# A slice's operand and weight loads in two pools by first need, gated second-stage loads, and last norms over 1024 columns

## The chip, the cores and the metric

One core of one Trainium2 chip runs the whole program. The metric is the device time of one execution in microseconds, median of the runs. TensorE multiplies, VectorE (DVE) and ScalarE (ACT) do elementwise work, GpSimd (POOL) and SyncE (SP) issue DMAs, each on a queue of its own.

## The reference

A block of a streaming encoder over 512 rows of 2048 columns in float32, one layer:

```python
h = layer_norm(x, ln_in_g, ln_in_b)
u = h @ W_in                                   # pool values | q | k | v
mix = concat(multi_scale_pool(u), stick_breaking_attention(q, k, v)) @ W_out
h = layer_norm(ALPHA * h + mix, ln1_g, ln1_b)
f = relu(h @ W_1 + b_1) ** 2                   # 2048 -> 8192, "FFN1"
f = f @ W_2 + b_2                              # 8192 -> 2048, "FFN2"
h = layer_norm(ALPHA * h + f, ln2_g, ln2_b)
```

## The kernel before

Float32 products are made of rounded parts: a matrix is split into a high part `th` (a cast on ACT, L756) and a low part `tl` (a subtract on DVE, L757), and three matmuls stand for one.

FFN1 runs in 16 blocks of 512 columns (`f0` to `f15`). `operands` squares each block's four PSUM banks on DVE into one tile `g` (`r15_0` to `r15_3` are the last block's activations), makes sums and differences of its quarters, and splits them into `fh` (ACT, L699) and `fl` (DVE, L700). POOL's queue stores them to a scratch in DRAM, `f_d[slice][unit]`, four stores of 896 KB a block (L702). Seven operands, numbered 0 to 6, come out of each block.

FFN2 runs in 4 slices (`slice_of`) of 4 units (blocks) each, as a product of two-by-two blocks with seven multiplications. In a slice the steps `one` and `five` go over units 0 and 1, then 2 and 3; then `six` and `three_` over the units, then `seven`, then `four` and `two`. Each step does two column halves (n = 0, 1), and one step of one unit and half is 12 matmuls of 128x512. Step one multiplies operand 0, five operand 3, six 4, three_ 6, seven 5, four 2 and two 1. Steps one, six, seven and four add into the PSUM banks `x`, five and three_ into `v`. In the traces a tile's name has lost its digits of slice and kind: `o` is any operand, `b` any raw unit of w2.

- Operands: `operand` (L735) loads 512 KB from `f_d` on SP's queue into a place of a ring of 16: four in pool `first`, twelve in `ring`. `o0_4_1` is slice 0, operand 4, unit 1.
- Weights: `w2_unit` (L746) loads 512 KB of w2 on SP's queue into one of ten raw places, three in `wp` and seven in `right`; they are called b11, b12, b22 and b21 by the quarter they come from. In slice 0 three units of step one take b11 and five adds b12 to it on DVE (L808, giving `c`); for the other units a chain `c` is loaded with b11 (L797), split for step one, and b12 is added in DRAM-to-SBUF by an accumulating DMA on POOL's queue (`add_unit`, L750). In six DVE adds b22 to the chain (L817), and three_ adds b12 to the raw tile by POOL's queue.
- The tile scheduler sets each engine's order from priorities (`tc.high_priority`) and the waits that pools imply. A queue runs in order: what is behind a waiting load waits too. A DMA of SP also waits for the one eight places before it.
- Pools `chains`, `right` and `ring` are opened after FFN1's pools are closed and lie over their space, so a first tile in them waits for the last readers of what lay there.

After each stage `every` adds PSUM to the accumulators `acc0` to `acc3` on DVE (L772). At the end `norm_out` normalizes each 128-row block `tb`: statistics (L928), then for each of four 512-column quarters one instruction with mean and scale (L932), one with the reciprocal deviation and bias (L933), and an output DMA (L934).

Of the kernel before, what the change touches and what calls it, by code (L numbers as in the profile page):

```python
# [9 lines left out]
F32 = mybir.dt.float32  # L10
F32R = mybir.dt.float32r
AF = mybir.ActivationFunctionType
ALU = mybir.AluOpType

P = 128
N = 512
# [7 lines left out]
def block_kernel(  # L24
# [18 lines left out]
    nc = tc.nc  # L43
# [4 lines left out]
    NT = S // P  # L48
    NQ = D // N
# [5 lines left out]
    out2 = out[0]  # L55
# [3 lines left out]
    def pool(stack, name, bufs, **kw):  # L59
        return stack.enter_context(tc.tile_pool(name=name, bufs=bufs, reuse_waits="tile", **kw))  # L60
# [6 lines left out]
    wp = pool(ctx, "wp", 2)  # L67
# [17 lines left out]
    def f(ap):  # L85
        return ap.bitcast(F32)

    def after(ins, earlier):

        tc.add_manual_dep(ins.ins, earlier.ins.name, mybir.DependencyInfo(  # L90
            mybir.DependencyClass.Sync, mybir.DependencyReason.DATA), reason="whole bank")
# [4 lines left out]
    def rows_tile(i, name, dt=F32):  # L96
        return rows.tile([P, NQ, N], dt, tag=f"y{i}", name=name)
# [182 lines left out]
    def three(bank, a, b, first, last, free=False):  # L280
        (ah, al), (bh, bl) = a, b
        for n, (l, r) in enumerate(((ah, bh), (ah, bl), (al, bh))):
            mm = nc.tensor.matmul(bank, l, r, start=first and n == 0, stop=last and n == 2, skip_group_check=free)  # L283
        return mm
# [246 lines left out]
    for half in range(2):  # L531
        if half:
            v_block(half)
        for pair in (2 * half, 2 * half + 1):
            parts = qk_block(pair)
# [6 lines left out]
    acc_t = [rows_tile(tb, f"acc{tb}") for tb in range(NT)]  # L542
    acc = [[acc_t[tb][:, q, :] for q in range(NQ)] for tb in range(NT)]
# [107 lines left out]
    for q in range(NQ):  # L651
        gb = tmp.tile([P, N], F32, tag="w", bufs=3, name=f"g1_{q}")
# [5 lines left out]
        for tb in range(NT):  # L658
            a = acc[tb][q]
# [11 lines left out]
    first = pool(ctx, "first", 4, side="right")  # L671
# [7 lines left out]
    f_d = [[scratch.tile([OPS, 2, P, N], F32, name=f"f_d{s}_{u}") for u in range(PER)] for s in range(NS)]  # L679
# [30 lines left out]
    late = ctx.enter_context(ExitStack())  # L710
    chains = pool(late, "chains", 1)
    right = pool(late, "right", 2)
    ring = pool(late, "ring", 12)
    ps = pool(late, "ps", 2, space=PSUM)
    used = {"op": 0, "raw": 0, "parts": 0}

    def turn(what, own, n):

        used[what] += 1
        return (used[what] - 1) % n < own  # L720

    def place(name, dt=F32R):

        at_first = turn("op", 4, 16)
        return (first if at_first else ring).tile([P, 2, N], dt, tag="o", bufs=4 if at_first else 12, name=name)

    rowsop = {}

    def operand(s, us, *os):

        with tc.high_priority(offset=400):
            for u in us:
                for o in os:
                    t = place(f"o{s}_{o}_{u}")
                    nc.sync.dma_start(f(t), f_d[s][u][o].rearrange("h p t -> p h t"))  # L735
                    rowsop[o, u] = t.rearrange("p h (i t) -> p h i t", i=2)

    def w2_at(b, half, q):

        k0 = b * N + half * H2  # L740
        return w2[k0:k0 + H2, q * N:(q + 1) * N].rearrange("(c p) n -> p c n", p=P)

    def w2_unit(b, half, q, name):
        early_one = turn("raw", 3, 10)
        raw = (wp if early_one else right).tile([P, 2, N], F32, tag="raw", bufs=3 if early_one else 7, name=name)
        nc.sync.dma_start(raw, w2_at(b, half, q))  # L746
        return raw

    def add_unit(t, b, half, q):
        nc.gpsimd.dma_start(t, w2_at(b, half, q), accum_op=ALU.add)  # L750

    def parts(t, name, ring=False):
        pl = wp if turn("parts", 2, 4) else right
        h = place(f"th_{name}") if ring else pl.tile([P, 2, N], F32R, tag="wh", bufs=2, name=f"th_{name}")
        l = place(f"tl_{name}") if ring else pl.tile([P, 2, N], F32R, tag="wl", bufs=2, name=f"tl_{name}")
        nc.scalar.copy(h, t)  # L756
        nc.vector.tensor_tensor(l, t, f(h), op=ALU.subtract)  # L757
        return h, l

    def times(banks, op, u, w, first, last, ts=(0, 1)):  # L760
        a, (wh, wl) = rowsop[op, u], w
        for i in range(2):
            for t in ts:
                ts_ = slice(t * P, (t + 1) * P)
                mm = three(banks[t], (a[:, 0, i, ts_], a[:, 1, i, ts_]), (wh[:, i, :], wl[:, i, :]),
                           first and i == 0, last and i == 1, True)
        return mm
# [9 lines left out]
    def slice_of(s):  # L777
# [2 lines left out]
        ahead = lambda: tc.high_priority(offset=400)  # L780
        units = range(PER)
        x = [pair(f"x{s}_{n}", f"x{n}") for n in range(2)]
        chain, b22, b11 = {}, {}, {}

        def step(n, u):
            return s * PER + u, f"{s}_{n}_{u}", (u == 0, u == PER - 1)
# [1 line left out]
        def one(n, u):  # L788
            b, at, e = step(n, u)
            with ahead():  # L790
                if s == 0 and 2 * u + n < 3:

                    b11[n, u] = w2_unit(b, 0, n, f"b11_{at}")
                    p1 = parts(b11[n, u], f"1_{at}")
                else:
                    c = chain[n, u] = chains.tile([P, 2, N], F32, tag=f"c{n}{u}", bufs=1, name=f"c_{at}")
                    nc.sync.dma_start(c, w2_at(b, 0, n))  # L797
                    p1 = parts(c, f"1_{at}")
                    add_unit(c, b, 0, n + 2)
            times(x[n], 0, u, p1, *e)  # L800

        def five(n, u):
            b, at, e = step(n, u)
# [8 lines left out]
        def six(n, u):  # L812
            b, at, _ = step(n, u)
            with ahead():
                b22[n, u] = w2_unit(b, 1, n + 2, f"b22_{at}")
                c = chain[n, u]
                nc.vector.tensor_tensor(c, c, b22[n, u], op=ALU.add)  # L817
                p6 = parts(c, f"6_{at}")
                if end:
                    add_unit(c, b, 1, n)  # L820
            times(x[n], 4, u, p6, False, u == PER - 1)
# [54 lines left out]
        every(x, 0, 0)  # L876
        every(v, 2, 2)
        for u in units:
            operand(s, (u,), 4, 6)
            both(six, (u,))  # L880
            both(three_, (u,))
        every(x, 0, 2)
# [31 lines left out]
    gb = {}  # L914

    def load_vectors():

        for n, vec in (("g", ln2_g[0]), ("b", ln2_b[0])):
            for i in range(2):
                t = place(f"ln2{n}{i}", F32)  # L920
                nc.sync.dma_start(t, vec.rearrange("(i q n) -> i q n", i=2, n=N)[i].partition_broadcast(P))
                for j in range(2):
                    gb[n, 2 * i + j] = t[:, j, :]

    def norm_out(tb):
        st = small.tile([P, NQ, 6], F32, name=f"st2_{tb}", tag="st")
        for q in (2, 3, 0, 1):
            nc.vector.bn_stats(st[:, q, :], acc[tb][q])  # L928
        mu, rs = finish_stats(st, f"n2{tb}", const)
        for q in range(NQ):  # L930
            a = acc[tb][q]
            nc.vector.scalar_tensor_tensor(a, a, mu, gb["g", q], op0=ALU.subtract, op1=ALU.mult)  # L932
            nc.vector.scalar_tensor_tensor(a, a, rs, gb["b", q], op0=ALU.mult, op1=ALU.add)  # L933
            nc.sync.dma_start(out2[tb * P:(tb + 1) * P, q * N:(q + 1) * N], a)  # L934

    for s in range(NS):
        slice_of(s)
# [33 lines left out]
```

## Time and profile before

| | us |
|---|---|
| median of three runs | 1992.52 |
| the three runs | 1992.07, 1992.52, 2177.56 |
| the profiled execution | 1992.84 |
| its span on the core | 1991.1 |
| TensorE busy in it | 1929.6 |

The page gives each engine's busy time and the share of the span. The trace gives each instruction's start and length, the idle time before it and what ended that, and the DMA issues with the time from issue to landing. A chain of waits follows the end of the program back, at each step to what released it.

### The profile page before, as it was taken

The numbers are of one execution on the slowest core, as the hardware profiler recorded it, in microseconds if no ns is written. First come the engines' busy times: TensorE is split into PE (matmuls) and PEld (weight loads), VectorE is DVE, ScalarE is ACT, GpSimd is POOL, SyncE is SP. The second block draws the span as 40 slices with busy tenths as digits, with TensorE's granted clock in tenths as the row PEclk, the third lists the DMA queues.
The fourth block names the chain that finished last, engine by engine and source line by source line (L and its number), as shares of the span: only waits on it lengthen the run. The fifth ranks groups of instructions, "written<-read, shape, count | busy, mean of one in ns | idle before, by whom it ended". The sixth has DMA issues, their size and how long they took to land.

```text
span 1991.1 us, 22343 instructions
## 1 busy us (share of the span) xinstructions
PE 1929.6 (97%) x8736; PEld 1596.0 (80%) x8736; DVE 1143.1 (57%) x1444; ACT 737.1 (37%) x898; POOL 168.4 (8%) x175
## 2 busy tenths in 40 slices
PE   6999999999999999999999999995999999999997
PEld 4888888887888988888888888873888888888885
DVE  8445565666458744444444444453666676675768
ACT  3344555552124233333333333331333333333341
POOL 5000000000000000000100000010101101100230
PEclk8999999999999999999999999996999999999999
DMA  6122222235344365555555555579788888888792
GB/s 223 33 85 85 74 86 84 76 105 184 107 148 122 130 219 180 170 169 169 203 205 184 169 169 169 170 259 356 179 290 226 189 275 239 184 264 274 184 218 85
DMA packets 171562, 345.48 MB, mean 174 GB/s; under 512 B 10688, under 2 KB 28224, under 8 KB 171072
## 3 DMA queue, kind: packets, MB, share of 16 engines
q1 hardware_dynamic: 137184, 249.07, 38.2%
q0 software_dynamic: 34128, 94.90, 18.1%
q8 instruction: 69, 1.13, 0.2%
q14 instruction: 37, 0.30, 0.1%
q10 hardware_dynamic: 144, 0.07, 0.0%
HBM read 281.09 MB, written 62.91 MB: 173 GB/s over the span
## 4 chain that ended last, share of the span: by engine, by line
PE 94%; DVE 3%; DMA 1%; SPq 1%; issue 1%; ACT 0%; DVEq 0%; ACTq 0%
PE f L210 33%; PE x L283 16%; PE qk L361 9%; PE v L283 9%; PE o L210 7%; PE p L210 4%; PE w L283 4%; PE o L283 3%; PE f L283 2%; PE v L210 2%; PE z L283 1%; PE v L276 1%; DMA o<-f_d 1%; PE v L274 1%; PE v L273 1%
## 5 line engine op out<-in xcount | busy, mean ns | idle before, releaser
L210 PE MATMUL f<-h1h,wh_f 128*128 128x512 f32 x960 | 373.5, 389 | 0.0
L210 PE MATMUL f<-h1l,wh_f 128*128 128x512 f32 x960 | 373.5, 389 | 0.0
L283 PE MATMUL x<-th,o 128*128 128x512 f32 x1024 | 325.8, 393 | 24.9 <-DMA o<-f_d 24.5
L210 PE MATMUL f<-h1h,wl_f 128*128 128x512 f32 x960 | 349.1, 389 | 0.0
L184 DVE TENSOR_TENSOR wl_f<-raw_f,wh_f 128x1024 fp32r<-128x1024 f32 x120 | 146.9, 1224 | 325.0 <-ACT wh_f L183 325.0
L183 ACT CAST wh_f<-raw_f 128x1024 fp32r<-128x1024 f32 x120 | 126.4, 1053 | 392.4 <-PE f L210 374.2
L283 PEld LDWEIGHTS x<-th,o 128*128 128x128 f32 x1024 | 193.3, 189 | 68.6 <-DMA o<-f_d 24.9
L757 DVE TENSOR_TENSOR tl<-c,th 128x1024 fp32r<-128x1024 f32 x125 | 152.2, 1224 | 130.2 <-ACT th L756 129.5
L756 ACT CAST th<-c 128x1024 fp32r<-128x1024 f32 x125 | 130.7, 1052 | 232.8 <-PE x L283 139.6
L210 PEld LDWEIGHTS f<-h1h,wh_f 128*128 128x128 f32 x960 | 180.3, 188 | 37.3
L210 PEld LDWEIGHTS f<-h1h,wl_f 128*128 128x128 f32 x960 | 180.2, 188 | 37.4
L210 PEld LDWEIGHTS f<-h1l,wh_f 128*128 128x128 f32 x960 | 180.2, 188 | 37.3
L283 PE MATMUL x<-tl,o 128*128 128x512 f32 x512 | 201.1, 393 | 0.3 <-DVE tl L757 0.3
L283 PE MATMUL v<-th,o 128*128 128x512 f32 x512 | 164.6, 395 | 3.1 <-ACT th L756 3.1
L756 ACT CAST th<-b 128x1024 fp32r<-128x1024 f32 x99 | 104.2, 1053 | 158.9 <-PE v L283 66.2
L757 DVE TENSOR_TENSOR tl<-b,th 128x1024 fp32r<-128x1024 f32 x99 | 120.7, 1222 | 70.0 <-ACT th L756 69.9
L702 POOL DMA_DIRECT2D f_d<-fh x32 | 30.9, 977 | 1193.6 <-ACT fh L699 1193.6
L283 PEld LDWEIGHTS v<-th,o 128*128 128x128 f32 x512 | 97.2, 190 | 25.0 <-ACT th L756 4.0
L283 PEld LDWEIGHTS x<-tl,o 128*128 128x128 f32 x512 | 96.6, 189 | 21.8 <-DVE tl L757 0.7
L283 PE MATMUL v<-tl,o 128*128 128x512 f32 x256 | 100.9, 394 | 0.0
L361 PE MATMUL qk<-hTl,wh_qk 128*128 128x512 f32 x256 | 99.9, 390 | 0.0
L361 PE MATMUL qk<-hTh,wh_qk 128*128 128x512 f32 x256 | 99.5, 390 | 0.0
(206 smaller groups left out, 3070.4 us busy)
## 6 DMA issues: line engine op xcount, KB each, us to landing
raw_f<-in_w_ff_dram SPq DMA_DIRECT2D x120, 512.0 KB, 3.9
o<-f_d SPq DMA_DIRECT2D x112, 512.0 KB, 6.4
b<-in_w_ff_dram SPq DMA_DIRECT2D x70, 512.0 KB, 5.5
f_d<-fh POOLq DMA_DIRECT2D x32, 896.0 KB, 6.0
f_d<-fl POOLq DMA_DIRECT2D x32, 896.0 KB, 9.6
c<-in_w_ff_dram POOLq DMA_DIRECT2D x37, 512.0 KB, 10.4
raw_qk<-in_w_in_dram SPq DMA_DIRECT2D x64, 256.0 KB, 2.9
b<-in_w_ff_dram POOLq DMA_DIRECT2D x32, 512.0 KB, 8.6
```

The costliest lines, as they stand in the source:

```text
L183: nc.scalar.copy(h, raw)
L184: nc.vector.tensor_tensor(l, raw, f(h), op=ALU.subtract)
L210: mm = nc.tensor.matmul(bank, a, b, start=first and n == 0, stop=last and n == 2)
L273: nc.tensor.matmul(bank, xh[kc][:, ts_], wh[n], start=n == 0, stop=False)
L274: nc.tensor.matmul(bank, xl[kc][:, ts_], wh[n], start=False, stop=False)
L276: mm = nc.tensor.matmul(bank, xh[kc][:, ts_], wl[n], start=False, stop=n == last)
L283: mm = nc.tensor.matmul(bank, l, r, start=first and n == 0, stop=last and n == 2, skip_group_check=free)
L361: nc.tensor.matmul(bank, a, b, start=kc == 0 and n == 0, stop=kc == KC - 1 and n == 2)
L702: nc.gpsimd.dma_start(f_d[b // PER][b % PER][:, n, :, i * H2:(i + 1) * H2].rearrange("o p t -> p o t"), f(t))
L756: nc.scalar.copy(h, t)
L757: nc.vector.tensor_tensor(l, t, f(h), op=ALU.subtract)
```

## The change

1. The place of an operand is taken from `first` (4), `ring_a` (4) and `ring_b` (8) instead of `first` (4) and `ring` (12); that of a raw unit from `wp` (3), `right` (3) and `raw_b` (4) instead of `wp` (3) and `right` (7). The number of places and their turn are the same; what they lie over is not.
2. In slice 0 the loads of six and three_ for unit u (operands 4 and 6, and b22) wait until the last matmul of the (4+u)-th step of one, in the order of the units and halves of `begun`: `begun[4]` and `[5]` are unit 2, `[6]` and `[7]` unit 3.
3. The last norms run over 1024 columns at a time, and all of the first instruction's pieces come ahead of the second's. Each block's output leaves in two DMAs, the last block's in four as before.

Lines of the changed kernel: L741 is L735 before, L754 is L746, L767 is L757, L807 is L797, L818 is L808, L827 is L817, L782 is L772, L937 is L928, L941 is L932 and L945 is L933.

```diff
     right = pool(late, "right", 2)
-    ring = pool(late, "ring", 12)
+    ring_a = pool(late, "ring_a", 4)
+    raw_b = pool(late, "raw_b", 4)
+    ring_b = pool(late, "ring_b", 8)
...
-    def turn(what, own, n):
-
+    def turn(what, *homes):
+
+        at = used[what] % sum(n for _, n in homes)
         used[what] += 1
-        return (used[what] - 1) % n < own
+        for home, n in homes:
+            if at < n:
+                return home, n
+            at -= n

     def place(name, dt=F32R):

-        at_first = turn("op", 4, 16)
-        return (first if at_first else ring).tile([P, 2, N], dt, tag="o", bufs=4 if at_first else 12, name=name)
+        home, n = turn("op", (first, 4), (ring_a, 4), (ring_b, 8))
+        return home.tile([P, 2, N], dt, tag="o", bufs=n, name=name)
...
-    def operand(s, us, *os):
+    def operand(s, us, *os, behind=None):
...
-                    nc.sync.dma_start(f(t), f_d[s][u][o].rearrange("h p t -> p h t"))
+                    load = nc.sync.dma_start(f(t), f_d[s][u][o].rearrange("h p t -> p h t"))
+                    if behind:
+                        after(load, behind)
...
-    def w2_unit(b, half, q, name):
-        early_one = turn("raw", 3, 10)
-        raw = (wp if early_one else right).tile([P, 2, N], F32, tag="raw", bufs=3 if early_one else 7, name=name)
-        nc.sync.dma_start(raw, w2_at(b, half, q))
+    def w2_unit(b, half, q, name, behind=None):
+        home, places = turn("raw", (wp, 3), (right, 3), (raw_b, 4))
+        raw = home.tile([P, 2, N], F32, tag="raw", bufs=places, name=name)
+        load = nc.sync.dma_start(raw, w2_at(b, half, q))
+        if behind:
+            after(load, behind)
...
-            times(x[n], 0, u, p1, *e)
+            begun.append(times(x[n], 0, u, p1, *e))
...
-                b22[n, u] = w2_unit(b, 1, n + 2, f"b22_{at}")
+                b22[n, u] = w2_unit(b, 1, n + 2, f"b22_{at}", begun[4 + u] if s == 0 else None)
...
-            operand(s, (u,), 4, 6)
+            operand(s, (u,), 4, 6, behind=begun[4 + u] if s == 0 else None)
...
-        for q in range(NQ):
-            a = acc[tb][q]
-            nc.vector.scalar_tensor_tensor(a, a, mu, gb["g", q], op0=ALU.subtract, op1=ALU.mult)
-            nc.vector.scalar_tensor_tensor(a, a, rs, gb["b", q], op0=ALU.mult, op1=ALU.add)
-            nc.sync.dma_start(out2[tb * P:(tb + 1) * P, q * N:(q + 1) * N], a)
+        for i in range(2):
+            a = acc_t[tb][:, 2 * i:2 * i + 2, :]
+            nc.vector.scalar_tensor_tensor(a, a, mu, gb["g", i], op0=ALU.subtract, op1=ALU.mult)
+        for i in range(2):
+            for j in range(2) if tb == NT - 1 else [slice(0, 2)]:
+                a, b = acc_t[tb][:, 2 * i:2 * i + 2, :][:, j], gb["b", i][:, j]
+                nc.vector.scalar_tensor_tensor(a, a, rs, b, op0=ALU.mult, op1=ALU.add)
+                to = out2[tb * P:(tb + 1) * P, :].rearrange("p (i j n) -> p i j n", i=2, n=N)[:, i]
+                nc.sync.dma_start(to[:, j], a)
```

SP in slice 0, before, from the last of FFN2's early loads to the operands of one and five for units 2 and 3 (`o0_0_2` to `o0_3_3`); the loads of b22, b21 and operand 5 above them have no reader until later stages (L746 and L735 as above):

```order
L735 DMA o0_5_1_10345<-f_d0_1_5518 128x2x512
L746 DMA b22_0_1_2_10170<-in_w_ff2_dram 128x2x512
L746 DMA b21_0_0_0_10455<-in_w_ff2_dram 128x2x512
L746 DMA b22_0_0_3_10227<-in_w_ff2_dram 128x2x512
L746 DMA b21_0_1_0_10474<-in_w_ff2_dram 128x2x512
L735 DMA o0_5_2_10379<-f_d0_2_5519 128x2x512
L735 DMA o0_5_3_10413<-f_d0_3_5520 128x2x512
L735 DMA o0_0_2_9839<-f_d0_2_5519 128x2x512
L735 DMA o0_3_2_9841<-f_d0_2_5519 128x2x512
L735 DMA o0_0_3_9843<-f_d0_3_5520 128x2x512
L735 DMA o0_3_3_9845<-f_d0_3_5520 128x2x512
```

SP in the changed kernel, from the last two chain loads on:

```order
L807 DMA c_0_0_3_9891<-in_w_ff2_dram 128x2x512
L807 DMA c_0_1_3_9910<-in_w_ff2_dram 128x2x512
L741 DMA o0_0_2_9845<-f_d0_2_5519 128x2x512
L741 DMA o0_3_2_9847<-f_d0_2_5519 128x2x512
L741 DMA o0_0_3_9849<-f_d0_3_5520 128x2x512
L741 DMA o0_3_3_9851<-f_d0_3_5520 128x2x512
L741 DMA o0_5_0_10317<-f_d0_0_5517 128x2x512
L741 DMA o0_5_1_10351<-f_d0_1_5518 128x2x512
L741 DMA o0_5_2_10385<-f_d0_2_5519 128x2x512
L741 DMA o0_5_3_10419<-f_d0_3_5520 128x2x512
L741 DMA o0_2_0_10457<-f_d0_0_5517 128x2x512
L754 DMA b22_0_0_0_10005<-in_w_ff2_dram 128x2x512
```

The four operands now follow the last chain `c`, ahead of operand 5 and of every b22 and b21.

DVE, before, at the end of FFN1: `tl_1` and `tl_5` are the low parts for steps one and five, `g15` and `fl15` are of the last FFN1 block, L808 makes the chains:

```order
L757 TENSOR_TENSOR tl_1_0_1_1_9747<-c_0_1_1_9744,th_1_0_1_1_9746 128x1024
L700 TENSOR_TENSOR fl15_0_9646<-g15_9628,fh15_0_9645 128x1792
L808 TENSOR_TENSOR c_0_0_0_9765<-b11_0_0_0_9690,b12_0_0_0_9763 128x1024
L700 TENSOR_TENSOR fl15_1_9652<-g15_9628,fh15_1_9651 128x1792
L808 TENSOR_TENSOR c_0_1_0_9785<-b11_0_1_0_9708,b12_0_1_0_9783 128x1024
L757 TENSOR_TENSOR tl_5_0_0_0_9768<-c_0_0_0_9765,th_5_0_0_0_9767 128x1024
L808 TENSOR_TENSOR c_0_0_1_9805<-b11_0_0_1_9726,b12_0_0_1_9803 128x1024
L757 TENSOR_TENSOR tl_5_0_1_0_9788<-c_0_1_0_9785,th_5_0_1_0_9787 128x1024
L817 TENSOR_TENSOR c_0_0_0_9765<-c_0_0_0_9765,b22_0_0_0_9999 128x1024
L757 TENSOR_TENSOR tl_5_0_0_1_9808<-c_0_0_1_9805,th_5_0_0_1_9807 128x1024
```

DVE in the changed kernel at the same place:

```order
L689 TENSOR_TENSOR g15_9628<-r15_3_9638 128x2x256
L767 TENSOR_TENSOR tl_1_0_1_1_9753<-c_0_1_1_9750,th_1_0_1_1_9752 128x1024
L818 TENSOR_TENSOR c_0_0_0_9771<-b11_0_0_0_9696,b12_0_0_0_9769 128x1024
L691 TENSOR_TENSOR g15_9628<-g15_9628 128x512
L818 TENSOR_TENSOR c_0_1_0_9791<-b11_0_1_0_9714,b12_0_1_0_9789 128x1024
L818 TENSOR_TENSOR c_0_0_1_9811<-b11_0_0_1_9732,b12_0_0_1_9809 128x1024
L692 SCALAR_TENSOR_TENSOR g15_9628<-g15_9628 128x512
L767 TENSOR_TENSOR tl_5_0_0_0_9774<-c_0_0_0_9771,th_5_0_0_0_9773 128x1024
L694 SCALAR_TENSOR_TENSOR g15_9628<-g15_9628 128x512
L767 TENSOR_TENSOR tl_5_0_1_0_9794<-c_0_1_0_9791,th_5_0_1_0_9793 128x1024
L700 TENSOR_TENSOR fl15_0_9646<-g15_9628,fh15_0_9645 128x1792
L700 TENSOR_TENSOR fl15_1_9652<-g15_9628,fh15_1_9651 128x1792
```

The three chains and two low parts of five now stand ahead of both `fl15`, which wait behind them.

DVE at the end of the program, before (accumulators, statistics and norms of the third and fourth row block):

```order
L772 TENSOR_TENSOR acc2_3676<-acc2_3676,x3_0_0_12899 128x512
L772 TENSOR_TENSOR acc2_3676<-acc2_3676,x3_1_0_12901 128x512
L928 BN_STATS st2_2_13989<-acc2_3676 128x6 x2
L161 BN_AGGR mv_n22_13994<-st2_2_13989 128x2
L163 TENSOR_SCALAR v_n22_13996<-mv_n22_13994 128x1
L932 SCALAR_TENSOR_TENSOR acc2_3676<-acc2_3676,mv_n22_13994,ln2g0_13699 128x512 x2
L932 SCALAR_TENSOR_TENSOR acc2_3676<-acc2_3676,mv_n22_13994,ln2g1_13701 128x512 x2
L772 TENSOR_TENSOR acc3_3677<-acc3_3677,x3_0_1_12900 128x512
L167 RECIPROCAL r_n22_14000<-sd_n22_13998 128x1
L928 BN_STATS st2_3_14069<-acc3_3677 128x6
```

DVE in the changed kernel at the same place:

```order
L782 TENSOR_TENSOR acc2_3676<-acc2_3676,x3_1_0_12907 128x512
L937 BN_STATS st2_2_13983<-acc2_3676 128x6
L782 TENSOR_TENSOR acc2_3676<-acc2_3676,x3_0_0_12905 128x512
L937 BN_STATS st2_2_13983<-acc2_3676 128x6
L782 TENSOR_TENSOR acc3_3677<-acc3_3677,x3_0_1_12906 128x512
L161 BN_AGGR mv_n22_13988<-st2_2_13983 128x2
L937 BN_STATS st2_3_14057<-acc3_3677 128x6
L163 TENSOR_SCALAR v_n22_13990<-mv_n22_13988 128x1
L941 SCALAR_TENSOR_TENSOR acc2_3676<-acc2_3676,mv_n22_13988,ln2g0_13705 128x1024
L941 SCALAR_TENSOR_TENSOR acc2_3676<-acc2_3676,mv_n22_13988,ln2g1_13707 128x1024
```

The add of `x3_0_1` into `acc3` and its statistics have moved ahead of the third block's norm, and each pair of norm instructions over 512 columns is one over 1024.

## Rows read from the trace of the kernel before

**Rows 1.** Page, head and part 1: busy us, share of the span, instructions.

```profile
span 1991.1 us, 22343 instructions
...
PE 1929.6 (97%) x8736; PEld 1596.0 (80%) x8736; DVE 1143.1 (57%) x1444; ACT 737.1 (37%) x898; POOL 168.4 (8%) x175
```

**Rows 2.** Timeline of PE: start, us, engine, line, operation [idle before, releaser].

```profile
1329.10 0.50 PE L283 MATMUL x<-th,o 128*128 128x512 f32 x1 [0.25 <-ACT r L686]
...
1341.31 0.74 PE L283 MATMUL v<-th,o 128*128 128x512 f32 x2 [0.74 <-ACT th L756]
1344.40 1.22 PE L283 MATMUL v<-th,o 128*128 128x512 f32 x2 [2.35 <-ACT th L756]
...
1382.33 0.79 PE L283 MATMUL x<-th,o 128*128 128x512 f32 x1 [24.49 <-DMA o<-f_d]
```

**Rows 3.** Windows: length, busy us of each engine, granted clock, DMA share, GB/s.

```profile
1340.00:1350.00 10.00, 6.90 (x19) 4.83 (x18) 10.00 (x10) 3.17 (x4) 2.02 (x3) 0.66 1.06 345
...
1360.00:1370.00 10.00, 0.00 (x0) 0.00 (x0) 0.18 (x1) 0.00 (x0) 1.18 (x1) 0.50 1.10 261
1370.00:1380.00 10.00, 0.00 (x0) 0.00 (x0) 0.00 (x0) 0.00 (x0) 0.00 (x0) 0.50 1.07 328
1380.00:1390.00 10.00, 7.67 (x23) 6.14 (x24) 1.22 (x1) 1.05 (x1) 0.00 (x0) 0.63 1.05 408
```

**Rows 4.** Chain of waits of that stretch: start, us, what.

```profile
1368.15 14.14 DMA o<-f_d
...
1406.97 5.21 PE x L283 x23
1412.18 5.44 PE v L283 x24
...
1450.27 25.11 PE x L283 x108
```

**Rows 5.** Timeline of SP: groups of issues by line.

```profile
1344.33 16.21 SPq L746 DMA_DIRECT2D b<-in_w_ff_dram  x4
1360.76 35.49 SPq L735 DMA_DIRECT2D o<-f_d  x16
```

**Rows 6.** Timeline of POOL: stores and accumulating adds issued.

```profile
1342.36 0.95 POOL L702 DMA_DIRECT2D f_d<-fl  x1 [1.29 <-DVE fl L700]
1352.59 1.26 POOL L750 DMA_DIRECT2D c<-in_w_ff_dram  x1 [9.29 <-DVE tl L757]
...
1360.48 1.18 POOL L750 DMA_DIRECT2D c<-in_w_ff_dram  x1 [1.61 <-DVE tl L757]
```

**Rows 7.** DMA issues: windows at 1342.4, 1352.5, 1360.5, and page part 6: KB, us to landing.

```profile
f_d<-fl POOLq DMA_DIRECT2D x1, 896.0 KB, 18.3
...
c<-in_w_ff_dram POOLq DMA_DIRECT2D x1, 512.0 KB, 12.0
...
c<-in_w_ff_dram POOLq DMA_DIRECT2D x1, 512.0 KB, 16.2
...
c<-in_w_ff_dram POOLq DMA_DIRECT2D x37, 512.0 KB, 10.4
```

**Rows 8.** Timeline of DVE at the handover.

```profile
1338.90 1.22 DVE L808 TENSOR_TENSOR c<-b,b 128x1024 f32<-128x1024 f32 x1
1340.04 2.02 DVE L700 TENSOR_TENSOR fl<-g,fh 128x1792 fp32r<-128x1792 f32 x1
1341.97 1.22 DVE L808 TENSOR_TENSOR c<-b,b 128x1024 f32<-128x1024 f32 x1
```

**Rows 9.** Timelines of DVE and PE at the end.

```profile
1972.13 2.73 DVE L932 SCALAR_TENSOR_TENSOR acc<-acc,mv_n,ln2g 128x512 f32<-128x512 f32 x4
...
1977.57 0.39 PE L283 MATMUL x<-th,o 128*128 128x512 f32 x1
```

**Rows 10.** Groups by line and form, DVE: busy us, mean ns of one, idle before.

```profile
L757 DVE TENSOR_TENSOR tl<-c,th 128x1024 fp32r<-128x1024 f32 x125 | 152.2, 1224 | 130.2 <-ACT th L756 129.5 <-PE v L283 0.4
...
L772 DVE TENSOR_TENSOR acc<-acc,x 128x512 f32<-128x512 f32 x64 | 41.6, 682 | 1.4 <-PE x L283 1.4
```

More of the change, by code (lines that the diff above doesn't have):

```diff
@@ L752, in parts @@
     def parts(t, name, ring=False):
-        pl = wp if turn("parts", 2, 4) else right
+        pl, _ = turn("parts", (wp, 2), (right, 2))
         h = place(f"th_{name}") if ring else pl.tile([P, 2, N], F32R, tag="wh", bufs=2, name=f"th_{name}")
@@ L782, in slice_of @@
         x = [pair(f"x{s}_{n}", f"x{n}") for n in range(2)]
-        chain, b22, b11 = {}, {}, {}
+        chain, b22, b11, begun = {}, {}, {}, []
         def step(n, u):
@@ L921, in load_vectors @@
                 nc.sync.dma_start(t, vec.rearrange("(i q n) -> i q n", i=2, n=N)[i].partition_broadcast(P))
-                for j in range(2):
-                    gb[n, 2 * i + j] = t[:, j, :]
+                gb[n, i] = t
     def norm_out(tb):
```

## Prediction

> **What bounds the kernel now.** The page comes first: TensorE is busy 97% of the span [rows 1], so a change can only take back the stretches in which it stands or runs slowly, or make new ones. The timeline of TensorE shows where FFN1 hands over to FFN2: step one of slice 0 begins at 1329.10, five begins with two short waits for ACT's `th` (0.74 and 2.35 us), and then there is a wait of 24.49 us that a load of `o` from `f_d` ends at 1382.33 [rows 2]. The windows say that the DMA engines are full in all of that time (share 1.05 to 1.10) and that the granted clock is 0.50 from 1360 to 1380, the lower level of 1.2 GHz, and is not whole again until after the wait (0.63 in the next ten) [rows 3]. The chain of waits shows the price: the load that ends the wait was issued at 1368.15 and landed 14.14 us later, and one and five of the third and fourth unit end at 1406.97, where six's matmuls into `x` begin [rows 4]. In full stride 24 matmuls take 5.44 us [rows 4], so a step (12) takes 2.72 and the 16 steps of one and five 43.5. They take 1406.97 − 1329.10 = 77.9. So **34.4 us** is all that the handover can give back.
>
> Why was that load so late? SP issues in order. Ahead of `o_0_2` stand 14 loads that nothing needs yet (8 b22, 2 b21, 4 o_5); SP is held 16.21 us at four of them, and the row that starts with o_5_2 begins only at 1360.76 [rows 5]. Meanwhile POOL's queue carries the last block's four `f_d` stores and four accumulating adds into `c`; the last store, issued at 1342.36, takes 18.3 us, and the adds issued at 1352.59 to 1360.48 take 12.0 to 16.2 [rows 6, 7]. They land at 1360.7, 1364.6 and 1376.7.
>
> **The loads that move.** Now the four operands (o_0_2, o_3_2, o_0_3, o_3_3) stand right behind the last `c`, ahead of those 14, and their places lie over space that needs only FFN1's last matmuls and the first g instructions. On loads alone the queues moved 408 GB/s [rows 3], 1.29 us for 512 KB (524,288 bytes). From 1329 SP has three b12, four `c` and four operands to bring: 11 × 1.29 = 14.2, so the last lands by some 1343 if alone, 1350 with POOL's share taken off. one(2..3) needs them from 1351 on (below), so the 24.49 us wait goes. I take nothing for it.
>
> **The first DVE work.** c (L808 before) of the first three chains now precedes the last block's g and fl chain. Before, c_0_0 came at 1338.90 and c_1_0 at 1341.97, behind fl instructions of 2 us [rows 8]; th and tl of five hung on them. Their loads (b12) also lead the `c` loads now. I take five's first two waits as gone, 0.74 + 2.35 = 3.1 us, and 0.5 us for tl_5_0_1, which still stands behind both fl. The price: fl and so the last two stores start some 4.7 us later (three c and two tl at a pitch of 1340.04 − 1338.90 = 1.14 us [rows 8] are 5.7, less about one of waits that went with them), on a POOL queue where the adds are behind them. one and five (0..1) then end at 1329.1 + 8 × 2.72 + 0.5 = 1351.4, and one(2..3), 10.9 us more, at about 1362 to 1363.
>
> **What is late next.** five(2..3) needs `c` after its add. The adds stand on POOL behind the four stores, and an add can be issued only after tl of step one has read `c`. In the trace three adds in a row landed 12.1 us apart in all, (1376.7 − 1364.6) / 3 = 4.0 us each [rows 6, 7], with SP's loads beside them. After the change stores start later, but for some microseconds before the gates (below) open the SP queue has little to send, so the stores go faster. These two I let cancel: the adds land at 1364, 1368, 1372 and 1376, as before. From below: the page's median for this add is 10.4 us over quieter stretches [rows 7], so issued at some 1350 to 1354 the last lands by 1366. The row from this place is the nearer, so I take 1376. th and tl of the last step need 1.1 + 1.2 us behind it and the step 2.72: five ends at about **1380.6** (1376 to 1386), where it was 1406.97. That is 26.4 us of the 34.4.
>
> **The gates and the second stage.** b22, o_4 and o_6 of slice 0 now wait for the beginning of one(2..3), unit by unit, and come behind o_5 and o_2_0 on SP. Queued behind the gated loads are b21 and the operands of the next stage. Every unit of six and three_ needs four loads and makes two adds while TensorE works 10.9 us. A load costs the DMA engines 1.29 us; an add with one load beside it 4.0, so an add alone 4.0 − 1.29 = 2.7: 4 × 1.29 + 2 × 2.7 = 10.6 us. That is the 10.9 almost exactly. Before, all b22 lay in SBUF by then, so this stage ran in step from 1406.97 to 1450.27 [rows 4]. Now the first b22 lands at some 1374, o_4_0 and o_6_0 at 1376 to 1378 (some five loads at the 4.05 us a load that SP keeps beside the adds [rows 5], then at 1.29), and c+=b22 and its parts follow five's accumulations on DVE, 1.14 to 1.22 us each. I charge 3.4 us for this first turn, two to three DVE instructions, as bound 0 to 5, and nothing for the units behind it, since 10.6 stays below 10.9. Six and three_ end at 1380.6 + 43.5 + 3.4 = 1427.5, where they ended at 1450.27. Gain **22.8 us**. Cover that can go: if a unit takes over 10.9, each of four units pays the difference.
>
> **The pools.** Two pools by first need keep the turn of 16 operand and 10 raw places, so slices 1 to 3 get the same orders but for neighbours that change places. TensorE runs there without waits of note; I take 0, and −1 to +2 as bound.
>
> **The tail.** Here DVE, not TensorE, sets the end: the last matmul starts at 1977.57 and the norms run on [rows 9]. A norm instruction over 512 columns has a pitch of (2.73 − 0.75) / 3 = 0.66 us [rows 9]. No row shows one over 1024; a subtract of 1024 takes 1224 ns against 682 for 512 [rows 10], 0.54 more, so I estimate 0.66 + 0.54 = 1.20 against 1.32 for two. Six pairs on the last stretch save 0.7. Against that, acc3's add of x_0_1 now stands ahead of the third block's aggregate: x_0_1 ends 24 matmuls before the end, at 1977.96 − 5.44 = 1972.5, and with 0.6 for the add the aggregate starts at 1973.1 and not 1971.8: 1.3 later, 0.6 of which is work that is only moved. Sum 1.3 − 0.6 − 0.7 = 0 (−1 to +1).
>
> **Sum.** The profiled execution took 1992.84 us (span 1991.1 and 1.7 around it), the median is 1992.52, so they are the same. 1992.84 − 22.8 + 0 = **1970.0**, 1.15% less.
>
> **Shares of the two queues.** While stores and adds ran, SP was held 16.21 us for four loads [rows 5], 4.05 us each, 129 GB/s, about a third of what the windows show. If the two queues shared evenly, POOL would have a half and not two thirds: an add 4.0 × 4/3 = 5.3 us, a store a third more too, and the last add, behind four of each, at about 1384; five would end some 8 us later, 2 of it won back by SP's faster loads: 1976 us. The rows are of this stretch, so I keep a third and two thirds, and leave the other a chance (e). The Trainium skill's page "DMA: Bandwidth & Descriptors", section "Queues, rings and completion order", says that an engine takes its queue rows in turn, a packet each, which would be case (e) if packets are alike; the trace so far disagrees with it.
>
> **Rivals.**
> (a) *The adds come early.* For it: SP's queue is nearly empty between o_3_3 and the gates. If the last lands by 1366, one(2..3) and five(2..3) run in step to 1351.4 + 21.8 = 1373.2, and 3.4 is charged on top: gain 1450.3 − 1420.1 = 30.2 less some DMA-bound turns (about 2): 1964 to 1965. Against it: gated loads start at 1354.
> (b) *The clock falls in the short waits.* In the trace it fell to half within a wait and stayed there for a part of the work after it (0.50, then 0.63) [rows 3]. five's four steps would wait some 1 to 4 us each for adds that land 4.0 apart. At half pace a step takes 5.44, four steps lose up to 10.9, of which the waits hide a part: I take 6.5 us, 1976.5. The Trainium skill's page "TensorE: Matmul & The Clock Gate", section "HAM oscillation — how this bites in real kernels", describes such groups of matmuls, each started at the lower clock after a DMA wait. Whether steps of 2.72 us with waits of 1 to 4 do so no row here shows; behind the waits of 0.74 and 2.35 us the ten microseconds from 1340 had a mean clock of 0.66 [rows 3], which speaks for it.
> (c) *Other side: the second stage starves.* If SP's loads keep the pace of 4.05 us beside adds, a unit of six and three_ takes 4 × 4.05 = 16.2 us, and with TensorE waiting in each step it stays at half clock, 5.1 to 5.4 us a step, 16 steps at least 82 us in place of 43.5: 1970 + 38.5, less the 3.4 charged above, is 2005. It decides against the change from 2.72 + 22.8 / 16 = 4.1 us a step. Against it: two adds a unit do not keep POOL's queue busy all the time.
> (d) *It doesn't do what it says:* o_0_2 held by something else ahead of it, a place not yet free: 24 us stay, and with the second stage's new gates it is 1985 to 1995.
>
> **Chances.** Sum as worked out 0.45 (1966.5 to 1974), (a) 0.20 (1959 to 1966), (b) 0.17 and (e) 0.07 (both 1974 to 1982), (d) 0.06, (c) 0.05. The range 1960 to 1982 takes these four, leaving out a little of each end. The floor is 1992.84 − 34.4 = 1958.4, so faster by over 2% (below 1952.7; 2% is about what a measurement of this kernel can tell from no change) needs a gain that no row shows: 0.02. Slower by over 2% (above 2032) is the far end of (c): 0.02. Within 2%: 0.96.
>
> **What would show it.** Timeline of TensorE: no wait of over 5 us for `o<-f_d`; one(2..3) ends by 1365; the next waits are of ACT's `th` behind POOL's adds, at 1360 to 1378. DMA issues: `c` adds land 4 us apart up to 1376. Windows: clock of 1360 to 1380 near 1.00 in my case, under 0.8 in (b). Chain: six and three_ end near 1427. I would be wrong if loads of b22 or o_4 ended waits in each unit of six, or if the adds landed ten microseconds earlier or later.

## The result, and the profile after

The changed kernel takes **1973.18 us** (median of four runs, 1972.30 to 1975.13) against 1992.52 before. That is the median of three runs; a fourth, of 2177.56, fell in a slower state of the chip and stands in no comparison. The ratio is 0.9902, with a 95% interval from 0.9885 to 0.9919: 1% faster, within 2%. The forecast was 1970 (1960 to 1982). The profiled execution took 1972.86, 20.0 less than that of before.

The page after, its head and its first row, answers to [rows 1]:

```profile
span 1971.2 us, 22308 instructions
...
PE 1929.7 (98%) x8736; PEld 1594.3 (81%) x8736; DVE 1141.0 (58%) x1430; ACT 736.5 (37%) x898; POOL 168.6 (9%) x175
```

TensorE is busy for the same time (1929.7 us, slowed matmuls included) in a span that is 20 us shorter, so what went was waiting.

The timeline of TensorE in the handover answers to [rows 2] (start, length, operation, and in brackets the idle time before it with what ended it). These are the waits but for two of 0.53 us for `tl`, at 1367.42 and 1380.65:

```profile
1347.55 0.51 PE L283 MATMUL v<-tl,o 128*128 128x512 f32 x1 [0.46 <-DVE tl L767]
...
1366.16 0.73 PE L283 MATMUL v<-th,o 128*128 128x512 f32 x2 [2.79 <-ACT th L766]
...
1375.53 0.50 PE L283 MATMUL v<-tl,o 128*128 128x512 f32 x1 [0.53 <-DVE tl L767]
...
1379.39 0.73 PE L283 MATMUL v<-th,o 128*128 128x512 f32 x2 [1.29 <-ACT th L766]
...
1413.32 0.50 PE L283 MATMUL v<-tl,o 128*128 128x512 f32 x1 [0.87 <-DVE tl L767]
```

No load of `o` from `f_d` ends a wait any more, and five begins without the 0.74 and 2.35 us. What is left stands at 1366.16, where ACT's `th` ends a wait of 2.79 us, and in short waits for `tl` and `th` up to 1381; one wait in three_ at 1413 is ended by DVE's `tl`. The step before the wait at 1366.16 is the last of one, so one ended at 1363.4.

The windows answer to [rows 3] (last three columns: granted clock, DMA share, GB/s):

```profile
1360.00:1370.00 10.00, 6.69 (x23) 4.86 (x23) 3.96 (x5) 1.92 (x2) 0.00 (x0) 0.86 1.10 268
1370.00:1380.00 10.00, 8.10 (x31) 5.45 (x30) 3.08 (x3) 2.93 (x4) 0.00 (x0) 0.97 1.08 311
1380.00:1390.00 10.00, 9.47 (x35) 7.58 (x35) 10.00 (x12) 4.38 (x5) 1.78 (x2) 0.83 1.06 393
```

The granted clock is 0.86, 0.97 and 0.83 in the three windows in which it was 0.50, 0.50 and 0.63, and the DMA engines are as full as before (share 1.06 to 1.10). The POOL timeline and the DMA issues of the last store and the four `c` adds answer to [rows 6, 7]:

```profile
1346.66 0.94 POOL L702 DMA_DIRECT2D f_d<-fl  x1 [0.53 <-DVE fl L700]
1348.93 1.26 POOL L760 DMA_DIRECT2D c<-in_w_ff_dram  x1 [1.33 <-DVE tl L767]
1351.20 1.21 POOL L760 DMA_DIRECT2D c<-in_w_ff_dram  x1 [1.01 <-DVE tl L767]
1352.80 1.19 POOL L760 DMA_DIRECT2D c<-in_w_ff_dram  x1 [0.38 <-DVE tl L767]
1358.32 1.18 POOL L760 DMA_DIRECT2D c<-in_w_ff_dram  x1 [4.34 <-DVE tl L767]
```

```profile
f_d<-fl POOLq DMA_DIRECT2D x1, 896.0 KB, 14.4
...
c<-in_w_ff_dram POOLq DMA_DIRECT2D x1, 512.0 KB, 16.1
...
c<-in_w_ff_dram POOLq DMA_DIRECT2D x1, 512.0 KB, 17.8
...
c<-in_w_ff_dram POOLq DMA_DIRECT2D x1, 512.0 KB, 20.3
...
c<-in_w_ff_dram POOLq DMA_DIRECT2D x1, 512.0 KB, 19.9
```

Issue plus time to landing gives 1361.1 for the last store and 1365.0, 1369.0, 1373.1 and 1378.2 for the adds. Stores are issued later than before and the adds earlier, and they land at nearly the same times.

In the chain of waits of the second stage (start, us, what) a load of b21 leads by way of DVE's `c` add (L859) to the wait at 1413; seven begins at 1429.56, where it was 1450.27 [rows 4]:

```profile
1387.05 23.83 DMA b<-in_w_ff_dram
...
1410.91 1.23 DVE c L859
...
1429.56 22.39 PE x L283 x96
```

### The profile page after: what moved, and what is told of

Same layout as the page of the kernel before. It is cut to its first block, busy times and chain, and to the rows that moved or that the text cites. A ratio compares the mean times of both kernels' runs of the same rounds, so it can differ in the third digit from the quotient of the medians.

```text
span 1971.2 us, 22308 instructions
## 1 busy us (share of the span) xinstructions
PE 1929.7 (98%) x8736; PEld 1594.3 (81%) x8736; DVE 1141.0 (58%) x1430; ACT 736.5 (37%) x898; POOL 168.6 (9%) x175
## 4 chain that ended last, share of the span: by engine, by line
PE 91%; DMA 3%; DVE 3%; issue 1%; SPq 1%; ACT 0%; POOL 0%; DVEq 0%; POOLq 0%; ACTq 0%
PE f L210 33%; PE x L283 15%; PE qk L361 9%; PE v L283 7%; PE o L210 7%; PE p L210 4%; PE w L283 4%; PE o L283 3%; DMA b<-in_w_ff_dram 3%; PE f L283 2%; PE v L210 2%; PE z L283 1%; PE v L276 1%; DMA f_d<-fl 1%; PE v L274 1%
## 5 line engine op out<-in xcount | busy, mean ns | idle before, releaser
L767 DVE TENSOR_TENSOR tl<-c,th 128x1024 fp32r<-128x1024 f32 x125 | 151.8, 1223 | 111.2 <-ACT th L766 110.6
L767 DVE TENSOR_TENSOR tl<-b,th 128x1024 fp32r<-128x1024 f32 x99 | 120.3, 1220 | 63.0 <-ACT th L766 62.9
```

## The experiments

Each kernel was timed in rounds beside the kernel before, on the same chip. The two on the norms were timed once.

**Without the gates.** Edit on the changed kernel:

```diff
-                b22[n, u] = w2_unit(b, 1, n + 2, f"b22_{at}", begun[4 + u] if s == 0 else None)
+                b22[n, u] = w2_unit(b, 1, n + 2, f"b22_{at}")
-            operand(s, (u,), 4, 6, behind=begun[4 + u] if s == 0 else None)
+            operand(s, (u,), 4, 6)
```

> The changed kernel without the gates: b22, o_4 and o_6 of slice 0 no longer wait for step one of units 2 and 3; pools and norms as changed. In SP's order the four operands (o0_0_2 to o0_3_3) keep their place behind the last chain c; five b22, two b21, four o_5 and two more operands come between them and b22_0_0_0. Theory 1 (the places under ring_a let the four operands go first, and the gates only sort what follows): no wait for o<-f_d, five ends at 1384 to 1386 as in the changed kernel, since the c adds still end at about 1378; six and three_ start at 1387 to 1390, behind those loads; time 1973 to 1978. Theory 2 (the gates carry the gain): time back near 1990.

1977.16 us, ratio to before 0.9921 (0.9906 to 0.9936). The two long waits of TensorE in the handover:

```profile
1366.95 1.22 PE L283 MATMUL v<-th,o 128*128 128x512 f32 x2 [3.22 <-ACT th L766]
...
1388.63 1.19 PE L283 MATMUL v<-th,o 128*128 128x512 f32 x2 [5.30 <-DMA o<-f_d]
```

The first is the wait for the adds, as in the changed kernel (the last add landed at 1378.3, the same as there). The second is new: at the start of the second stage `o_6_0`, behind fourteen other loads on SP, is 5.30 us late. Five ended at 1383.3, 1.3 us earlier than in the changed kernel, so the 5.30 us cost about 4. Theory 1 holds, but for this one wait for an operand, which it didn't have. The pools alone let the four operands go first; the gates are worth the other 4 us, because they decide which loads come next.

**Without the new pools.** Edit on the changed kernel:

```diff
-    ring_a = pool(late, "ring_a", 4)
-    raw_b = pool(late, "raw_b", 4)
-    ring_b = pool(late, "ring_b", 8)
+    ring = pool(late, "ring", 12)
...
-        home, n = turn("op", (first, 4), (ring_a, 4), (ring_b, 8))
+        home, n = turn("op", (first, 4), (ring, 12))
...
-        home, places = turn("raw", (wp, 3), (right, 3), (raw_b, 4))
+        home, places = turn("raw", (wp, 3), (right, 7))
```

> The changed kernel with the old two pools (right 7, ring 12): gates and norms as changed. In SP's order three o_5 loads stand ahead of the four operands, and these lie again over FFN1's stage and wait for its stores (the last landed at 1360.7 to 1361.1 in both kernels). Theory A (the c adds on POOL's queue set the end of five, whatever the operands do up to some 1372): o0_0_3 lands at about 1366, step one of unit 3 ends at 1372, the adds end at 1376 to 1378 and five at 1383 to 1387: time 1973 to 1978, though the operands land some 20 us later than in the changed kernel. Theory B (the operands' landing sets it): 15 to 20 us of the gain are lost, time 1988 to 1993.

1978.32 us, ratio 0.9926 (0.9910 to 0.9943). TensorE's waits, and from the DMA issues the last `c` add (issued at 1360.96):

```profile
1341.68 0.73 PE L283 MATMUL v<-th,o 128*128 128x512 f32 x2 [0.75 <-ACT th L764]
1344.77 1.22 PE L283 MATMUL v<-th,o 128*128 128x512 f32 x2 [2.36 <-ACT th L764]
...
1359.58 0.47 PE L283 MATMUL x<-th,o 128*128 128x512 f32 x1 [1.26 <-DMA o<-f_d]
...
1368.69 0.76 PE L283 MATMUL x<-th,o 128*128 128x512 f32 x1 [3.40 <-DMA o<-f_d]
```

```profile
c<-in_w_ff_dram POOLq DMA_DIRECT2D x1, 512.0 KB, 13.6
```

The time is 0.3 us above what theory A said, the reason holds only in part. The last add landed at 1374.6 and was not waited for; TensorE waited 1.26 and 3.40 us for operands, was slow after the wait of 3.40 (24 matmuls in 8.2 us, granted clock 0.78 from 1370 to 1380), and five ended at 1387.8. So here the operands set the end, 3 us later than the adds set it in the changed kernel. The operands landed 15 to 22 us later than in the changed kernel and cost 5 us of time, since the adds leave five little more to win. The waits of 0.75 and 2.36 us at the head of five are back, too: without the new pools b12 stands behind the `c` loads and DVE makes the chains behind `fl` again. With the new norms in both, gates alone give 14.6 us of the 19 to 20, pools alone 15.8; either keeps the needed loads from standing behind all 14.

**The loads of the next stages held back.** Edit on the changed kernel:

```diff
-                operand(s, (u,), 5)
+                operand(s, (u,), 5, behind=begun[7] if s == 0 else None)
...
-                operand(s, (u,), 2, 1)
+                operand(s, (u,), 2, 1, behind=begun[7] if s == 0 else None)
```

> The changed kernel, and also operands 5, 2 and 1 of slice 0 wait for the last step of one. Four o_5 and o_2_0 no longer stand between the four operands and the first b22. Theory (loads that nothing needs yet still share the DMA engines with the stores and adds between 1350 and 1374): the last c add lands 2 to 4 us earlier, at 1374 to 1376, b22_0_0_0 lands ten microseconds or more before its use, and six and three_ end at 1424 to 1427: time 1968 to 1971. Rival (the adds run at 4.0 us each on POOL's queue whatever SP loads): last add at 1378, time 1973 within 1.

1971.78 us, ratio 0.9891 (0.9877 to 0.9906). TensorE's wait at the head of five (2..3), and from the DMA issues the last add, issued at 1358.5:

```profile
1367.59 0.73 PE L283 MATMUL v<-th,o 128*128 128x512 f32 x2 [3.38 <-ACT th L766]
```

```profile
c<-in_w_ff_dram POOLq DMA_DIRECT2D x1, 512.0 KB, 16.5
```

It landed at 1375.0, 3.2 us earlier than in the changed kernel, with nothing of POOL's own order changed: what SP loads in that time does slow the stores and adds. Five ended 2 us earlier, but the stage behind it lost this again and ended at 1429.7 (forecast 1424 to 1427): DVE waited until 1411.5 for b21, which now came behind four o_5, with low parts of three_ and six behind that add, and TensorE waited 3.39 us for one of them. The median is 1.4 us under the changed kernel's, and the intervals of the two ratios overlap: the effect on the adds is shown, that on the whole is not.

**The last block's stores on another queue.** Edit on the changed kernel:

```diff
-                nc.gpsimd.dma_start(f_d[b // PER]...
+                (nc.scalar if b == BLOCKS - 1 else nc.gpsimd).dma_start(f_d[b // PER]...
```

> The changed kernel with the last FFN1 block's four stores to f_d issued by ACT on its queue, so that the c adds no longer stand behind them on POOL's. Theory (the adds are late because of the queue they share with the stores): c adds, issued at 1349 to 1358, land 10 to 12 us after issue, the last at 1366 to 1370, five ends at 1372 to 1377, and six and three_ at 1418 to 1424: time 1962 to 1968. Rival (the DMA engines as a whole are full, and it does not matter which queue carries the stores): last add at 1376 or later, time 1972 to 1976.

1974.74 us, ratio 0.9911 (0.9896 to 0.9926), no gain. ACT's timeline (ACTq: its DMA issues), and from the DMA issues the first `c` add, issued at 1351.7:

```profile
1345.60 3.40 ACTq L702 DMA_DIRECT2D f_d<-fl  x1
...
1349.18 7.83 ACTq L702 DMA_DIRECT2D f_d<-fl  x1
1357.05 2.94 ACT L766 CAST th<-c 128x1024 fp32r<-128x1024 f32 x3 [6.90 <-issue]
```

```profile
c<-in_w_ff_dram POOLq DMA_DIRECT2D x1, 512.0 KB, 8.7
```

The first add landed 8.7 us after its issue and not 16.1: without the stores ahead of it on its queue this add was fast. But ACT, which issues the stores now, was held 3.40 and 7.83 us at two of them (by what, the trace does not show), the casts behind them came late, the other three adds were issued only at 1360.8 to 1364.8 and the last landed at 1377.0. Five ended 2 us earlier than in the changed kernel all the same, and the next stage lost it in waits of 0.95 and 3.27 us for `tl`. By its numbers the rival came out. But the run shows the cost of the shared queue for one add only, and it doesn't tell what free adds would bring, since it made new waits.

**The four late adds to `c` off POOL's queue.** The edit of the run before last, the gates of unit u at `begun[6 + u // 2]`, and:

```diff
                     p1 = parts(c, f"1_{at}")
-                    add_unit(c, b, 0, n + 2)
+                    if s == 0 and u > 1:
+                        b12 = w2_unit(b, 0, n + 2, f"b12_{at}")
+                        nc.vector.tensor_tensor(c, c, b12, op=ALU.add)
+                    else:
+                        add_unit(c, b, 0, n + 2)
```

> The gates on operands 5, 2 and 1 as in the run before, the gates of b22, o_4 and o_6 a step later (units 0 and 1 at the third, 2 and 3 at the last unit of step one), and for units 2 and 3 of slice 0 b12 is loaded by SP and added to the chain c on DVE, in place of the accumulating add on POOL's queue. No c add then stands behind the last block's stores. Theory (five of units 2 and 3 waits only for those adds, and its half clock comes from these waits): no wait of over 1 us before five ends, which is 1329.1 + 16 x 2.72 + 1 to 2 = 1374 to 1376, granted clock 1.00 from 1350 to 1390, six and three_ end at 1418 to 1421, time 1961 to 1965. Rival (the DMA engines as a whole are behind by then and the next loads become late instead): five ends at 1380 or later, or six waits for b22 and o_4; time 1969 or more.

1966.62 us, ratio 0.9870 (0.9854 to 0.9887). Windows, the three waits of TensorE and DVE's timeline before the last of them:

```profile
1360.00:1370.00 10.00, 8.10 (x34) 5.83 (x33) 10.00 (x11) 4.20 (x4) 0.00 (x0) 1.00 0.97 347
1370.00:1380.00 10.00, 10.00 (x46) 8.28 (x45) 10.00 (x11) 4.22 (x4) 0.00 (x0) 1.00 1.05 404
1380.00:1390.00 10.00, 10.00 (x45) 8.27 (x45) 10.00 (x11) 4.22 (x4) 2.48 (x2) 1.00 1.08 326
```

```profile
1364.68 0.73 PE L283 MATMUL v<-th,o 128*128 128x512 f32 x2 [0.95 <-ACT th L766]
...
1369.27 0.50 PE L283 MATMUL v<-tl,o 128*128 128x512 f32 x1 [0.95 <-DVE tl L767]
...
1411.48 0.50 PE L283 MATMUL x<-tl,o 128*128 128x512 f32 x1 [1.80 <-DVE tl L767]
```

```profile
1403.76 1.23 DVE L863 TENSOR_TENSOR c<-c,b 128x1024 f32<-128x1024 f32 x1 [5.10 <-DMA b<-in_w_ff_dram]
...
1409.07 1.22 DVE L863 TENSOR_TENSOR c<-c,b 128x1024 f32<-128x1024 f32 x1 [2.95 <-DMA b<-in_w_ff_dram]
1410.21 2.35 DVE L767 TENSOR_TENSOR tl<-c,th 128x1024 fp32r<-128x1024 f32 x2
```

Waits of 0.95 us are all that is left in five, the clock is 1.00 from 1360 to 1390, and five ended at 1377.1 with two matmuls of six already among its own: the waits and the half clock of the changed kernel hung on the adds. The gates on operands 5, 2 and 1 alone left a wait of 3.38 us, in the run before last; the later gates for b22, o_4 and o_6 were not run alone, so their part isn't shown. The second half of the forecast failed by 3 us. DVE waited 5.10 and 2.95 us for b21 (the add of L863), and `tl` for six of unit 3 stood behind it; TensorE lost 3.7 us there (seven begins at 1424.07, in the next run at 1420.39), the slow matmuls behind the wait included.

**That add put behind three_.** Edit on the run before, where `done` holds the last matmul of each three_:

```diff
-                    nc.vector.tensor_tensor(c, c, b21, op=ALU.add)
+                    add = nc.vector.tensor_tensor(c, c, b21, op=ALU.add)
+                    if s == 0:
+                        after(add, done[-1])
```

> The run with the DVE adds, and c += b21 of slice 0 on DVE (the step of four) is put behind the last matmul of three_, so that no low part for six and three_ stands behind it. There DVE stood until b21_0_1_0 landed at 1409.0 and TensorE lost 3.7 us in six of unit 3. Theory (the 3.7 us come from that order on DVE, not from late b22 or operands): no wait in six and three_ of over 0.7 us, they end at 1420 to 1421 instead of 1423.9, time 1962 to 1964. Rival (the loads of the last units are late as well): six waits for th or tl of unit 3 anyway, time 1966 or more.

**1963.81 us**, ratio 0.9855 (0.9839 to 0.9871), the fastest of all. The chain of the second stage is TensorE alone, in full stride (5.44 us for 24), and seven begins at 1420.39:

```profile
1409.51 5.44 PE x L283 x24
1414.94 5.45 PE v L283 x24
1420.39 22.39 PE x L283 x96
```

The 3.7 us came from DVE's order, and in this stage nothing took their place. 2.8 of them reach the median.

**That one edit on the changed kernel** (the add of b21 behind three_).

> The changed kernel with that one edit alone (c += b21 of slice 0 behind the last matmul of three_); c adds, gates, pools and norms as in the changed kernel. In the changed kernel the wait in three_ of unit 2 was 1.2 us. Theory (five's end at 1384.6 and TensorE's pace set the rest): that wait goes, six and three_ end at 1428.2, time 1971 to 1973. Rival (the second stage is paced by the DMA engines): another wait takes its place, for b22 or o_4 of units 2 and 3, and they end at 1429.4 or later.

1970.87 us, ratio 0.9890 (0.9875 to 0.9904). Timelines of TensorE and DVE:

```profile
1412.12 0.50 PE L283 MATMUL v<-tl,o 128*128 128x512 f32 x1 [1.25 <-DVE tl L767]
```

```profile
1409.71 1.23 DVE L827 TENSOR_TENSOR c<-c,b 128x1024 f32<-128x1024 f32 x1 [5.65 <-DMA b<-in_w_ff_dram]
```

Here the rival's mechanism holds, though not its number. The wait for b21 is gone, and one of the same kind stands in its place: DVE waits 5.65 us for a b22 that lands at 1409.7, with the same `tl` behind it, and TensorE waits 1.25 us. From the end of five to the end of three_ it took 45.4 us, in the changed kernel 44.8 and in full stride 43.5. Three_ ended at 1428.4 and not at the rival's 1429.4, since in the profiled execution five ended 1.6 us earlier than in the changed kernel's, which this edit does not touch; so the median, 2.3 us lower with intervals that overlap, is no gain that the edit is shown to bring. So with loads that come as late as here, the next late one takes the place of the one that was moved; in the run before, the last b22 landed at 1384.9, 25 us earlier, and the same edit was worth its 3.7 us.

**The norms alone.** First the changed kernel with the old norms, then the kernel before with the new ones:

```diff
-        for i in range(2):
-            a = acc_t[tb][:, 2 * i:2 * i + 2, :]
-            nc.vector.scalar_tensor_tensor(a, a, mu, gb["g", i], op0=ALU.subtract, op1=ALU.mult)
...
+        for q in range(NQ):
+            a = acc[tb][q]
+            nc.vector.scalar_tensor_tensor(a, a, mu, gb["g", q // 2][:, q % 2], op0=ALU.subtract, op1=ALU.mult)
...
```

> The changed kernel with the old last norms (512 columns an instruction, four output DMAs a block). The sum had the tail at 0 (-1 to +1): from the end of the last matmul to the end of the span 13 to 14 us with either; time within 1.5 us of the changed kernel.

> The kernel before with only the new norms (1024 columns an instruction, two output DMAs for the first three blocks). All up to the last stage as before, the wait of 24.5 us included; the end from the last matmul on within 1 us of the kernel before; time 1991 to 1994. A norm instruction over 1024 columns has a pitch of 1.20 us (estimate of the sum: 0.66 + 0.54).

One run of each took 1971.79 and 1991.27. At the end of the program: the last matmul on TensorE and the last norms on DVE, for the changed kernel, then the same two views with the old norms, then for the kernel before with the new:

```profile
1957.13 0.39 PE L283 MATMUL x<-th,o 128*128 128x512 f32 x1
```

```profile
1964.10 2.74 DVE L945 SCALAR_TENSOR_TENSOR acc<-acc,rs_n,ln2b 128x512 f32<-128x512 f32 x4
```

```profile
1956.51 0.39 PE L283 MATMUL x<-th,o 128*128 128x512 f32 x1
```

```profile
1963.72 2.74 DVE L942 SCALAR_TENSOR_TENSOR acc<-acc,rs_n,ln2b 128x512 f32<-128x512 f32 x4
```

```profile
1975.80 0.39 PE L283 MATMUL x<-th,o 128*128 128x512 f32 x1
```

```profile
1982.78 2.74 DVE L935 SCALAR_TENSOR_TENSOR acc<-acc,rs_n,ln2b 128x512 f32<-128x512 f32 x4
```

From the last matmul's start to the last group of norms it is 6.97 and 6.98 us with the new norms and 7.21 and 7.20 with the old (before: 1977.57 [rows 9] to 1984.77). To the end of the span it is 14.0 and 13.8 with the new, 13.6 and 13.6 with the old; in the seven other kernels with the new norms it is 13.8 to 14.1. DVE is 0.23 us sooner done and the span ends 0.2 to 0.5 later. The norms move nothing that the times can show; why the end of the span came later was not tried.

## Why the prediction was right, step by step

- **The loads that move.** Right: the four operands landed at 1344.6 to 1350.9 (forecast 1343 to 1350), and no wait for `o<-f_d` is left. Rival (d) did not come.
- **The first DVE work.** Right: 0.46 us for tl_5_0_1 (forecast 0.5), both longer waits gone, the last store 4.3 us later (forecast 4.7). One ended at 1363.4 (1362 to 1363). That it hangs on the pools shows in the run without them, where both waits came back.
- **What is late next.** Right in kind and nearly in size: the adds landed 1.0, 1.0, 1.1 and 2.2 us after the forecast, and TensorE waited for them; they were not early, as rival (a) had them. Five ended at 1384.6 and not 1380.6. 2.2 us of these 4.0 are the last add. The other 1.8 are rival (b), of which a part came: the last step took from 1379.39 to 1384.6, 5.2 us with a wait of 0.53 for `tl` in it, where 2.72 was put behind `tl`. Of the three steps before it, the first ran at half pace too, but what it lost was covered by the waits for the next adds. So 1.8 us, not 6.5. The windows of 0.86 and 0.97 lie between the two signs given for the clock (near 1.00, under 0.8).
- **Shares of the two queues.** The pace held, the reading of it did not. The adds landed 4.0, 4.0 and 5.1 us apart, the last at 1378, where an even split of the time (e) had 1384. The page "DMA: Bandwidth & Descriptors" of the Trainium skill, section "Queues, rings and completion order", names turns by packet. The prediction took this for case (e) and against the trace; the packets in the trace of the kernel before agree with the page. Its DMA view has POOL's queue (software) and SP's (hardware), first with the stores, from 1350 to 1360, then with the adds, from 1362 to 1374 (packets, MB, and the time of the packets as a share of the 16 engines' time):

```profile
q0 software_dynamic: 713, 2.63, 68.1%
q1 hardware_dynamic: 708, 1.36, 35.8%
```

```profile
q0 software_dynamic: 814, 1.57, 70.5%
q1 hardware_dynamic: 814, 1.57, 39.3%
```

Each queue got as many packets as the other. POOL's two thirds are of the time: the stores' packets are larger (3.7 KB against 1.9), and those of the adds, as large as SP's, take 1.8 times as long. In bytes SP has a third beside the stores and a half beside the adds.

- **The gates and the second stage.** The charge of 3.4 us for the first turn was too much, for three_ went first and TensorE went on without a wait. 1.3 us came in its stead, nearly all at 1413, for b21 by way of DVE, which the sum had not. Six and three_ ended at 1429.4, forecast 1427.5. The estimate of 10.6 us of DMA work in 10.9 of TensorE's fits: the DMA share is 1.06 to 1.10 in all windows from 1380 to 1430, and the stage waits a little wherever one load is moved. It runs clean with the four adds off POOL's queue and the add of b21 behind three_. Starving, rival (c), did not come.
- **Pools, tail.** From the start of seven to the last matmul it took 527.5 before (1450.1 to 1977.57) and 527.7 after; behind the last matmul 0.5 more. The norm over 1024 columns has a mean of 1276 ns and a pitch of 1.19, estimated 1.20.
- **Sum.** Gain 20.7 in the handover and second stage (forecast 22.8), 0.7 lost behind it (forecast 0): 20.0. The path was right; that the sum came within 3 us of the result is in part luck. Five came 4.0 us late, the second stage lost 1.3 at a place that the sum had not, and the 3.4 charged for its first turn, which wasn't needed, made up for most of it.

The handover's floor leaves another 13.7 us. The two kernels with the adds off POOL's queue took back 9.2 of them (seven begins at 1420.39 in the faster one): five's long waits and the half clock went with the adds, together with the changed gates, and 3.7 more with DVE's order. The other 4.5 stay; five still ended about that much behind full stride, at 1377.1. Of the two causes of the late adds, the queue shared with the stores and the DMA engines shared with SP's loads, each has a run that shows it (8.7 for 16.1 us of an add; the last add 3.2 us earlier); how the time splits between them stays open.

## What to carry to other kernels

When a load is late, read what stands ahead of it on its queue, and then write down what will be late next: here the accumulating adds on another queue, whose landing times could be taken from the trace of the kernel before, bounded a saving of 24.5 us to 20. The accumulating DMAs behind large stores paid for their place in the queue, and plain loads with an add on an engine that had time were worth 6.5 us more together with later gates and gates on the next stages' loads, 9.4 with DVE's order mended. An edit that only reorders pays where it frees the last thing waited for; the same edit was worth 3.7 us of its stage in one kernel, and no gain of it is shown in another. To reckon how two queues share, count packets: the bytes and the time follow from what a packet of each carries and takes.

## What the runs showed of the hardware

An issue of a DMA by ACT held ACT itself, 3.40 and 7.83 us at two stores, with the casts behind them idle for 4.13 and 6.90. Beside each other, POOL's queue and SP's sent equal numbers of packets, 713 and 708 with stores, 814 and 814 with adds. An accumulating DMA's packets took 1.8 times the time of a load's of the same size (70.5% against 39.3% of the engines' time). Half the clock after short waits cost time only behind the last wait here: in the changed kernel the windows stood at 0.86, 0.97 and 0.83, and 1.8 us were lost.
